# Row tiles leave PSUM by a copy and an adding DMA; the copies of y into PSUM go

## The chip, the cores and the metric

One core of a Trainium2 chip. The metric is the device time of one execution in microseconds (us). A core has five engines with a queue of their own: PE (matmul, with its weight loads listed as PEld), DVE (elementwise), ACT (copies and activations), POOL and SP, which mostly issue DMAs. PSUM holds the matmuls' sums in eight banks of 128 x 512 float32; SBUF holds everything else.

## The reference

A transformer layer over 256 positions of width 2048, float32, with two SwiGLU feed-forward halves around a mixer:

```python
def _swiglu(x, w_gate, w_up, w_down):
    return (jax.nn.silu(x @ w_gate) * (x @ w_up)) @ w_down
def _macaron_ffn(x, pre_g, w_gate, w_up, w_down, post_g):
    return x + 0.5 * _rms_norm(_swiglu(_rms_norm(x, pre_g), w_gate, w_up, w_down), post_g)
...
h = _macaron_ffn(h, ffn1...)       # D_MODEL 2048, D_FF 5632
h = _gated_mixers(h, ...)          # attention, Fourier mix, gates, output projection
h = _macaron_ffn(h, ffn2...)
```

The change lies in the two feed-forward halves alone.

## The kernel before

Every float32 product is made of three matmuls (`mm3`, lines 109 to 111): each operand is split into a high part (ACT, line 103, `whi`) and a low part (DVE, line 104, `wlo`). A split takes one piece of weights, 128 x 1024, which SP loads into one of five `raw` buffers (line 84).

A feed-forward half has its 5632 inner columns in 11 blocks of 512. The first two are done plainly. For each further block f, `ffn` feeds two things to a queue, `Line`:

- the **round**, the down-projection of an earlier block's h: y (256 x 2048) += h (256 x 512) @ w_down. It has four column blocks `cb` of 512 and, in each, two row tiles t = 0, 1 of 128 x 512, one PSUM bank each, two pieces of weights per column block. In class `Rows`, `seed(cb, t)` takes a bank and copies y into it (ACT, line 661, `pr<-y`), the matmuls add to it, and `out` copies it back to y (ACT, line 679, `y<-pr`). The seeds of a column block are issued at the first piece of the one before it.
- `swiglu`, gate and up of block f. Six of its eight pairs of weight rows use seven products in place of eight (`seven`); their weights are differences of loaded pieces (DVE, line 582, tile `t13`). Two pairs are plain. Sums in the banks p1, p5, p6, p7, g0, g1, u0, u1 (all eight banks, named `pc` in the trace) are put together at the end by the lists `sums` (with `copy` of p1 to x1 on ACT, line 591), `gates` and `ups` (DVE, lines 587 and 599; ACT, line 595), and leave the banks free for the next round.

`Line` keeps up to ten pieces ahead of PE (`RING` 6 and `RING_B8` 4; six in the last block): `feed` first pops the oldest entry (its matmuls, then its `then` list), then prepares the new one (load and split). An entry with `hold` lets the next feed's preparation wait for one step. DVE, ACT and PE run the loop in exactly the order in which it is written, so an ACT or DVE instruction that waits holds up all that stand behind it on its engine. PSUM has two pools: five banks `pmm` and three `ptr`. Work tiles (x1, x2, x3, x5) come from a pool of eight, `wk`.

At `cb == 3` of a round, the h of the block just finished is transposed on PE for the next round (`ahead`). There are ten such rounds in each half; the first has nothing to add to, the last is followed by `last_rows`, which does the eleventh block.

Of the kernel before, what the change touches and what calls it, by code (L numbers as in the profile page):

```python
# [10 lines left out]
F32 = mybir.dt.float32  # L11
# [3 lines left out]
AF = mybir.ActivationFunctionType  # L15
# [3 lines left out]
P = 128  # L19
D = 2048  # L20
# [37 lines left out]
def encoder_layer(  # L58
# [298 lines left out]
    def cbs(a, cb):  # L357
        return a[:, cb * NB:(cb + 1) * NB]
# [148 lines left out]
    def ring(src):  # L507

        n = src.shape[1]
        i = turn["n"] = (turn["n"] + 1) % (RING + RING_B8)  # L510
        if turn["more"] and i % 5 in (1, 3):
            both = big("w2", F32R, [P, 2, WP, NB])
            hi, lo = both[:, 0], both[:, 1]
        else:
            hi = wring.tile([P, WP, NB], F32R, tag="hi", name="whi")
            lo = wring.tile([P, WP, NB], F32R, tag="lo", name="wlo")
        split(hi[:, 0:n, :], lo[:, 0:n, :], src)
        return [(hi[:, i, :], lo[:, i, :]) for i in range(n)]

    def raw_piece(src, i):  # L520
        raw = wraw.tile([P, WP, NB], F32, tag="raw", name="raw")
        load(raw[:], src.rearrange("p (i k c) -> p i k c", k=WP, c=NB)[:, i])
        return raw
# [31 lines left out]
            while self.queue:  # L555
                self.next()

    def swiglu(line, forms, w, hs, seed):


        ps, begun, x = {}, set(), {}

        def mul(n, a, b, last=False):
            if n not in ps:
                ps[n] = ptr.tile([P, NB], F32, tag="tr", name="pc") if n in ("p5", "p7", "p1") else                     pmm.tile([P, NB], F32, tag="mm", name="pc")
            mm3(ps[n][:], *a, *b, n not in begun, last)
            begun.add(n)

        def raw(pair, i):
            return raw_piece(w[pair // 2], pair % 2 * 2 + i)  # L570

        def plain(pair, i, *then, hold=False):
            def use(b):
                for t in range(NT):
                    for j in range(2):
                        k = 2 * pair + j
                        mul("gu"[i] + str(t), forms.plain[k][t], b[j], k == KD - 1)

            line.feed(lambda: ring(raw(pair, i)[:]), use, *then, hold=hold)

        def minus(out, a, b):
            V.tensor_tensor(out=out, in0=a, in1=b, op=ALU.subtract)  # L582

        def add(out, a, b):
            if out not in x:
                x[out] = work(out)
            V.tensor_tensor(out=x[out][:], in0=ps[a][:], in1=x[b][:], op=ALU.add)  # L587

        def copy():
            x["x1"] = work("x1")  # L590
            A.activation(x["x1"][:], ps["p1"][:], AF.Copy)

        def silu(t):
            g = x["x" + "13"[t]]
            A.activation(g[:], g[:], AF.Silu)  # L595

        def times(t):
            g, up = x["x" + "13"[t]], x["x" + "25"[t]]
            V.tensor_tensor(out=up[:], in0=up[:], in1=g[:], op=ALU.mult)
            hs.append(up)  # L600

        def seven(pair, between=None, *then):
            a11, a12, na22, s1, s2, s3, s4 = forms.seven[pair]
# [12 lines left out]

            def second():
                b = ring(h["t"][:])
                minus(h["t"][:, 0, :], h["ra"][:, 1, :], h["rb"][:, 1, :])
                return b  # L620

            def two(n, a, m, b, last):
                def use(ws):
                    mul(n, a, ws[0], last)
                    mul(m, b, ws[1], last)
                return use

            line.feed(first, two("u0", s4, "g0", a12, False))
            line.feed(second, two("p5", s1, "p7", s3, end))
            if between:  # L630
                between()
            line.feed(lambda: ring(h["ra"][:]), two("p1", a11, "p6", s2, end), *then[0:4], hold=end)
            line.feed(lambda: ring(h["t"][:, 0:1, :]), lambda ws: mul("g1", na22, ws[0]), *then[4:], hold=end)

        sums = [copy, lambda: seed(0, ptr, "tr"), lambda: add("x2", "p6", "x1"), lambda: seed(1),
                lambda: add("x3", "p7", "x2"), lambda: add("x2", "p5", "x2"), lambda: add("x5", "p5", "x3")]
        gates = [lambda: add("x1", "g0", "x1"), lambda: add("x3", "g1", "x3"), lambda: silu(0), lambda: silu(1)]
        ups = [lambda: add("x2", "u0", "x2"), lambda: times(0), lambda: add("x5", "u1", "x5"), lambda: times(1)]
        for kg in range(KD // CK):
            a, b = 2 * kg, 2 * kg + 1  # L640
            if kg == KD // CK - 1:
                seven(a, None, *sums)
                plain(b, 0, *gates, hold=True)
                plain(b, 1, *ups)
            elif b in BY_SEVEN:
                seven(a)
                seven(b)
            else:
                seven(a, lambda: plain(b, 0))
                plain(b, 1)  # L650

    class Rows:


        def __init__(self, w, rb, y, first):
            self.w, self.rb, self.y, self.first, self.ps = w, rb, y, first, {}

        def seed(self, cb, t, pool=pmm, tag="mm"):
            self.ps[cb, t] = pool.tile([P, NB], F32, tag=tag, name="pr")
            if not self.first:  # L660
                A.activation(self.ps[cb, t][:], cbs(self.y[t], cb), AF.Copy)  # L661

        def feed(self, line, ch, ahead):

            def use(b, cb, i):
                if i == 0:
                    if cb in ahead:
                        ahead[cb]()
                    for t in range(NT if cb + 1 < D // NB else 0):
                        self.seed(cb + 1, t)  # L670
                for t in range(NT):
                    for j in range(WP):
                        k = i * WP + j
                        mm3(self.ps[cb, t][:], ch[0][:, k, t * P:(t + 1) * P], ch[1][:, k, t * P:(t + 1) * P], *b[j],
                            self.first and k == 0, k == CK - 1, not self.first)

            def out(cb):
                for t in range(NT):
                    A.activation(cbs(self.y[t], cb), self.ps[cb, t][:], AF.Copy)

            for cb in range(D // NB):
                for i in range(CK // WP):
                    line.feed(lambda i=i, cb=cb: ring(raw_piece(self.w[self.rb, cb], i)[:]),
                              lambda b, i=i, cb=cb: use(b, cb, i), *([lambda cb=cb: out(cb)] if i == CK // WP - 1 else []))

    def ffn(u, rs, wg, wu, wgu, wd, yname, tail, gate0, w_next=None, early=()):

# [29 lines left out]
        with tc.manual_schedule(engines={mybir.EngineType.DVE, mybir.EngineType.Activation, mybir.EngineType.PE}):  # L717
            for f in range(PLAIN, nblk + 1):
                if f == nblk:
                    norm, nxt = tail(y)  # L720

                def ahead(hs=hs, f=f):
                    chs.append(new_chunk("hT")) if f > PLAIN else None
                    turn_h(chs[-1], hs)

                before = {D // NB - 1: ahead}
                if f == PLAIN:
                    before[0] = lambda: forms.chunk(KD // CK - 1)
                if f == PLAIN:
                    rows = Rows(wd, 0, y, True)  # L730
                    for t in range(NT):
                        rows.seed(0, t)
                rows.feed(line, chs[-1] if f > PLAIN else chs[0], before)
                if f < nblk:
                    hs = []
                    rows = Rows(wd, f - 1, y, False)
                    turn["more"] = f < nblk - 1
                    swiglu(line, forms, wgu[f - PLAIN], hs, lambda t, *room, rows=rows: rows.seed(0, t, *room))
            line.end()
        return last_rows(chs[-1], wd, nblk - 1, y, norm, nxt, w_next), nxt  # L740

# [616 lines left out]
```

## Time and profile before

| | |
|---|---|
| median of 3 runs | 2140.59 us (2136.44 to 2143.92) |
| the profiled execution | 2148.34 us, its span 2146.6 us |
| mean granted PE clock | 0.971 |
| PE, DVE, ACT, POOL busy | 95%, 83%, 63%, 1% of the span |
| DMA | 417.46 MB, mean 194 GB/s |

A row of the trace names the line, the engine, the operation, and out<-in by tile names. `L661` is a line of this kernel. "Idle before" and the waits name the instruction that ended an engine's idle time. PEclk is the share of its full clock that PE was granted. Line numbers are those of the kernel before; in the changed one, the copies out are on lines 675 and 678, the adding DMA on 679, the last round's add on 681.

### The profile page before, as it was taken

What the parts mean: (1) busy time and instruction counts of PE and PEld (TensorE: products, weight loads), DVE (VectorE), ACT (ScalarE), POOL (GpSimd) and SP (SyncE); (2) the same over time, 40 slices, a digit from 0 to 9 for tenths busy, and PEclk for the clock granted to TensorE, in tenths of its full rate; (3) what the DMA queues carried; (4) which work ended last, traced back from release to release, by engine and by line L of the source; (5) the groups of instructions that cost most, each with busy time, mean ns of one, the idle gap of its engine ahead of it and who ended that gap; (6) DMA issues with size and microseconds to landing.
All of it is one profiled execution on the core that took longest, in us unless ns stands there. A gap on an engine that the chain in (4) does not pass through costs nothing.

```text
span 2146.6 us, 26154 instructions
## 1 busy us (share of the span) xinstructions
PE 2032.8 (95%) x9146; PEld 1669.9 (78%) x9146; DVE 1790.8 (83%) x2416; ACT 1360.3 (63%) x1940; POOL 28.6 (1%) x30
## 2 busy tenths in 40 slices
PE   9998889888989999999999999999899889988998
PEld 7877778777878778888888888888677777777876
DVE  6898898889888888876877895888888889888895
ACT  7666666666666766555666655655656665666666
POOL 0000000000000010100000000000000000000002
PEclk9999999999999999999999999999999999999999
DMA  8564565446547686864555557565554555455653
GB/s 315 188 195 156 176 214 180 149 163 216 179 148 258 228 264 215 243 213 143 185 192 183 185 181 272 194 206 168 191 184 159 174 189 186 159 179 189 234 191 134
DMA packets 118741, 417.46 MB, mean 194 GB/s; under 512 B 12969, under 2 KB 19121, under 8 KB 116433
## 3 DMA queue, kind: packets, MB, share of 16 engines
q1 hardware_dynamic: 114256, 411.66, 57.1%
q0 software_dynamic: 4352, 4.13, 1.3%
q8 instruction: 72, 1.18, 0.2%
q14 instruction: 61, 0.49, 0.1%
HBM read 409.44 MB, written 6.29 MB: 194 GB/s over the span
## 4 chain that ended last, share of the span: by engine, by line
PE 62%; DVE 25%; DMA 5%; ACT 4%; issue 3%; SPq 0%; DVEq 0%; ACTq 0%
PE pc L110 11%; PE pc L111 11%; PE pc L109 11%; DVE wlo L104 10%; PE pr L109 8%; PE pr L110 8%; PE pr L111 8%; DVE t L582 4%; DVE w L104 4%; DVE x L587 3%; DMA raw<-in_f_down 3%; ACT whi L103 2%; DVE raw L582 1%; PE pt L179 1%; ACT x L595 1%
## 5 line engine op out<-in xcount | busy, mean ns | idle before, releaser
L104 DVE TENSOR_TENSOR wlo<-raw,whi 128x1024 fp32r<-128x1024 f32 (+1 forms) x560 | 677.1, 1219 | 152.9 <-ACT whi L103 150.3
L103 ACT ACTIVATE whi<-raw 128x1024 fp32r<-128x1024 f32 (+1 forms) x560 | 585.3, 1055 | 298.6 <-PE pc L111 126.8
L109 PE MATMUL pc<-whi,uh 128*128 128x512 f32 x688 | 272.6, 396 | 0.8 <-ACT uh L764 0.8
L110 PE MATMUL pc<-wlo,uh 128*128 128x512 f32 x688 | 270.4, 393 | 0.8 <-DVE wlo L104 0.8
L111 PE MATMUL pc<-whi,ul 128*128 128x512 f32 x688 | 270.2, 393 | 0.0
L109 PE MATMUL pr<-whi,hTh 128*128 128x512 f32 x492 | 206.3, 419 | 63.7 <-ACT pr L661 63.5
L110 PE MATMUL pc<-wlo,fh 128*128 128x512 f32 x626 | 244.4, 390 | 1.2 <-DVE wlo L104 1.0
L109 PE MATMUL pc<-whi,fh 128*128 128x512 f32 x626 | 243.9, 390 | 0.7 <-DVE hTl L104 0.7
L111 PE MATMUL pc<-whi,fl 128*128 128x512 f32 x626 | 243.8, 389 | 0.0
L582 DVE TENSOR_TENSOR t<-raw 128x512 f32<-128x512 f32 x324 | 213.6, 686 | 3.8
L104 DVE TENSOR_TENSOR w<-raw,w 128x1024 fp32r<-128x1024 f32 x151 | 184.3, 1220 | 29.1 <-ACT w L103 28.5
L103 ACT ACTIVATE w<-raw 128x1024 fp32r<-128x1024 f32 x151 | 159.2, 1054 | 68.7 <-DMA raw<-in_f_down 21.9
L110 PE MATMUL pr<-wlo,hTh 128*128 128x512 f32 x492 | 201.4, 409 | 0.0
L111 PE MATMUL pr<-whi,hTl 128*128 128x512 f32 x492 | 200.9, 408 | 0.0
L103 ACT ACTIVATE whi<-t 128x1024 fp32r<-128x1024 f32 (+1 forms) x138 | 117.0, 848 | 99.2 <-DVE t L582 88.5
L109 PEld LDWEIGHTS pr<-whi,hTh 128*128 128x128 f32 x492 | 98.6, 200 | 92.9 <-ACT pr L661 71.1
L104 DVE TENSOR_TENSOR wlo<-t,whi 128x1024 fp32r<-128x1024 f32 (+1 forms) x138 | 132.0, 957 | 44.8 <-ACT whi L103 44.8
L109 PEld LDWEIGHTS pc<-whi,uh 128*128 128x128 f32 x688 | 130.1, 189 | 28.2 <-ACT uh L764 2.5
L110 PEld LDWEIGHTS pc<-wlo,uh 128*128 128x128 f32 x688 | 130.0, 189 | 28.0 <-DVE wlo L104 2.8
L111 PEld LDWEIGHTS pc<-whi,ul 128*128 128x128 f32 x688 | 129.9, 189 | 27.0
L110 PEld LDWEIGHTS pc<-wlo,fh 128*128 128x128 f32 x626 | 117.5, 188 | 27.9 <-DVE wlo L104 3.7
L109 PEld LDWEIGHTS pc<-whi,fh 128*128 128x128 f32 x626 | 117.5, 188 | 26.0 <-issue 0.8
(361 smaller groups left out, 3609.4 us busy)
## 6 DMA issues: line engine op xcount, KB each, us to landing
raw<-in_f_gu SPq DMA_DIRECT2D x288, 512.0 KB, 4.5
raw<-in_f_down SPq DMA_DIRECT2D x176, 512.0 KB, 5.3
raw<-in_w_in SPq DMA_DIRECT2D x112, 512.0 KB, 4.7
raw<-in_f_up SPq DMA_DIRECT2D x32, 512.0 KB, 4.7
raw<-in_w_ao SPq DMA_DIRECT2D x32, 512.0 KB, 4.0
raw<-in_w_out SPq DMA_DIRECT2D x32, 512.0 KB, 4.4
raw<-in_f_gate SPq DMA_DIRECT2D x31, 512.0 KB, 5.8
fraw<-in_w_f SPq DMA_DIRECT2D x16, 512.0 KB, 6.1
```

Of the source, the lines that this page charges most:

```text
L103: a = A.activation(hi, src, AF.Copy)
L104: v = V.tensor_tensor(out=lo, in0=src, in1=hi.bitcast(F32), op=ALU.subtract)
L109: T.matmul(ps, lh, rh, start=first, stop=False, skip_group_check=onto)
L110: T.matmul(ps, lh, rl, start=False, stop=False, skip_group_check=onto)
L111: return T.matmul(ps, ll, rh, start=False, stop=last, skip_group_check=onto)
L179: T.transpose(pt[:, j, :], src[:, j * P:(j + 1) * P], ident[:])
L582: V.tensor_tensor(out=out, in0=a, in1=b, op=ALU.subtract)
L587: V.tensor_tensor(out=x[out][:], in0=ps[a][:], in1=x[b][:], op=ALU.add)
L595: A.activation(g[:], g[:], AF.Silu)
```

## The change

The seeds go. The round's matmuls start a fresh sum in their bank. What leaves the bank goes to y in one of three ways: the first round copies it to y on ACT (as before); rounds two to nine copy it on ACT to a new tile `part` from the pool `wk`, and a DMA issued on POOL adds `part` to y in SBUF; the tenth adds it to y on DVE. Banks are now taken at a column block's own first piece, and by a table: tiles (0,0), (1,0) and (1,1) from `ptr`, where p1, p7 and p5 were, the others from `pmm`. The lists of the last `seven` are cut elsewhere: two entries of `sums` follow its third piece, which no longer holds, the rest follows the fourth.

```diff
-    def swiglu(line, forms, w, hs, seed):
+    def swiglu(line, forms, w, hs):
...
-            line.feed(lambda: ring(h["ra"][:]), two("p1", a11, "p6", s2, end), *then[0:4], hold=end)
-            line.feed(lambda: ring(h["t"][:, 0:1, :]), lambda ws: mul("g1", na22, ws[0]), *then[4:], hold=end)
-
-        sums = [copy, lambda: seed(0, ptr, "tr"), lambda: add("x2", "p6", "x1"), lambda: seed(1),
-                lambda: add("x3", "p7", "x2"), lambda: add("x2", "p5", "x2"), lambda: add("x5", "p5", "x3")]
+            line.feed(lambda: ring(h["ra"][:]), two("p1", a11, "p6", s2, end), *then[0:2])
+            line.feed(lambda: ring(h["t"][:, 0:1, :]), lambda ws: mul("g1", na22, ws[0]), *then[2:], hold=end)
+
+        sums = [copy, lambda: add("x2", "p6", "x1"), lambda: add("x3", "p7", "x2"), lambda: add("x2", "p5", "x2"),
+                lambda: add("x5", "p5", "x3")]
...
-        def seed(self, cb, t, pool=pmm, tag="mm"):
-            self.ps[cb, t] = pool.tile([P, NB], F32, tag=tag, name="pr")
-            if not self.first:
-                A.activation(self.ps[cb, t][:], cbs(self.y[t], cb), AF.Copy)
...
+    def row_line(line, ch, w, rb, y, way, ahead):
+        rooms = {(0, 0): (ptr, "tr"), (1, 0): (ptr, "tr"), (1, 1): (ptr, "tr")}
+        for cb in range(D // NB):
+            ps = []
+            def use(b, i, cb=cb, ps=ps):
+                if i == 0:
+                    if cb in ahead:
+                        ahead[cb]()
+                    for t in range(NT):
+                        pool, tag = rooms.get((cb, t), (pmm, "mm"))
+                        ps.append(pool.tile([P, NB], F32, tag=tag, name="pr"))
...
+            def out(t, cb=cb, ps=ps):
+                dst = cbs(y[t], cb)
+                if way == "set":
+                    A.activation(dst, ps[t][:], AF.Copy)
+                elif way == "dma":
+                    part = work("part")
+                    A.activation(part[:], ps[t][:], AF.Copy)
+                    nc.gpsimd.dma_start(dst, part[:], accum_op=ALU.add)
+                else:
+                    V.tensor_tensor(out=dst, in0=ps[t][:], in1=dst, op=ALU.add)
...
+                way = "set" if f == PLAIN else "dma" if f < nblk else "add"
+                row_line(line, chs[-1] if f > PLAIN else chs[0], wd, f - 2, y, way, before)
```

ACT at the border between a block and its round, in the middle of the first half, before: the copy of p1, the two seeds of column block 0, two silus, four splits (`whi`, `w2` are split weights, `t13` the differences), the seeds of column block 1, and the first copies out.

```order
L591 ACTIVATE x1_3659<-pc_3396 128x512
L661 ACTIVATE pr_3661<-y0_941 128x512
L661 ACTIVATE pr_3665<-y1_942 128x512
L595 ACTIVATE x1_3659<-x1_3659 128x512
L595 ACTIVATE x3_3670<-x3_3670 128x512
L103 ACTIVATE whi_3709<-raw_3707 128x1024
L103 ACTIVATE w2_3715<-raw_3713 128x1024
L103 ACTIVATE whi_3725<-raw_3720 128x1024
L103 ACTIVATE whi_3730<-t13_3722 128x1024
L661 ACTIVATE pr_3735<-y0_941 128x512
L661 ACTIVATE pr_3737<-y1_942 128x512
L103 ACTIVATE w2_3751<-raw_3718 128x1024
```

The same place on ACT now:

```order
L591 ACTIVATE x1_3691<-pc_3428 128x512
L103 ACTIVATE whi_3697<-raw_3695 128x1024
L595 ACTIVATE x1_3691<-x1_3691 128x512
L595 ACTIVATE x3_3704<-x3_3704 128x512
L103 ACTIVATE w2_3743<-raw_3741 128x1024
L103 ACTIVATE whi_3753<-raw_3748 128x1024
L103 ACTIVATE whi_3758<-t13_3750 128x1024
L103 ACTIVATE w2_3777<-raw_3746 128x1024
L678 ACTIVATE part_3792<-pr_3763 128x512
L678 ACTIVATE part_3795<-pr_3764 128x512
L103 ACTIVATE whi_3798<-t13_3750 128x512
```

No copy from y is left, one split stands between the copy of p1 and the silus, and the copies out write `part`.

DVE at the same border, before: the last split ahead of the sums, the first five sums.

```order
L104 TENSOR_TENSOR w2_3650<-raw_3648,w2_3650 128x1024
L587 TENSOR_TENSOR x2_3663<-pc_3400,x1_3659 128x512
L587 TENSOR_TENSOR x3_3670<-pc_3388,x2_3663 128x512
L587 TENSOR_TENSOR x2_3663<-pc_3384,x2_3663 128x512
L587 TENSOR_TENSOR x5_3673<-pc_3384,x3_3670 128x512
L587 TENSOR_TENSOR x1_3659<-pc_3375,x1_3659 128x512
```

And now:

```order
L104 TENSOR_TENSOR w2_3682<-raw_3680,w2_3682 128x1024
L587 TENSOR_TENSOR x2_3693<-pc_3432,x1_3691 128x512
L104 TENSOR_TENSOR wlo_3698<-raw_3695,whi_3697 128x1024
L587 TENSOR_TENSOR x3_3704<-pc_3420,x2_3693 128x512
L587 TENSOR_TENSOR x2_3693<-pc_3416,x2_3693 128x512
L587 TENSOR_TENSOR x5_3707<-pc_3416,x3_3704 128x512
```

One split has moved from behind the sums to behind the first of them; the rest of DVE's order in the block is the same. PE's order doesn't change. POOL, which issued nothing in the feed-forward halves, now issues eight of these per round (the first two of a round are shown):

```order
L679 DMA y0_941<-part_3792 128x512
L679 DMA y1_942<-part_3795 128x512
```

They stand in the order of the copies on ACT, whose tiles they read.

More of the change, by code (lines that the diff above doesn't have):

```diff
@@ L650, in swiglu @@
                 plain(b, 1)
-    class Rows:
-        def __init__(self, w, rb, y, first):
-            self.w, self.rb, self.y, self.first, self.ps = w, rb, y, first, {}
-        def seed(self, cb, t, pool=pmm, tag="mm"):
-            self.ps[cb, t] = pool.tile([P, NB], F32, tag=tag, name="pr")
-            if not self.first:
-                A.activation(self.ps[cb, t][:], cbs(self.y[t], cb), AF.Copy)
-        def feed(self, line, ch, ahead):
-            def use(b, cb, i):
+    def row_line(line, ch, w, rb, y, way, ahead):
[3 more added lines that the diff above has]
+            def use(b, i, cb=cb, ps=ps):
                 if i == 0:
@@ L668, in use @@
                         ahead[cb]()
-                    for t in range(NT if cb + 1 < D // NB else 0):
-                        self.seed(cb + 1, t)
+                    for t in range(NT):
+                        pool, tag = rooms.get((cb, t), (pmm, "mm"))
+                        ps.append(pool.tile([P, NB], F32, tag=tag, name="pr"))
                 for t in range(NT):
@@ L673, in use @@
                         k = i * WP + j
[L674 to L684, printed above, removed]
+                        mm3(ps[t][:], ch[0][:, k, t * P:(t + 1) * P], ch[1][:, k, t * P:(t + 1) * P], *b[j],
+                            k == 0, k == CK - 1)
+            def out(t, cb=cb, ps=ps):
[8 more added lines that the diff above has]
+                    V.tensor_tensor(out=dst, in0=ps[t][:], in1=dst, op=ALU.add)
+            for i in range(CK // WP):
+                line.feed(lambda i=i, cb=cb: ring(raw_piece(w[rb, cb], i)[:]), lambda b, i=i, use=use: use(b, i),
+                          *([lambda t=t, out=out: out(t) for t in range(NT)] if i == CK // WP - 1 else []))
     def ffn(u, rs, wg, wu, wgu, wd, yname, tail, gate0, w_next=None, early=()):
@@ L728, in ffn @@
                     before[0] = lambda: forms.chunk(KD // CK - 1)
[L729 to L733, printed above, removed]
+                way = "set" if f == PLAIN else "dma" if f < nblk else "add"
+                row_line(line, chs[-1] if f > PLAIN else chs[0], wd, f - 2, y, way, before)
                 if f < nblk:
                     hs = []
-                    rows = Rows(wd, f - 1, y, False)
                     turn["more"] = f < nblk - 1
-                    swiglu(line, forms, wgu[f - PLAIN], hs, lambda t, *room, rows=rows: rows.seed(0, t, *room))
+                    swiglu(line, forms, wgu[f - PLAIN], hs)
             line.end()
```

## The prediction

> **What bounds the kernel now.** I read the page first, then the waits, then a table of stretches, then the timeline of one block border.
>
> ```profile
> PE 2032.8 (95%) x9146; PEld 1669.9 (78%) x9146; DVE 1790.8 (83%) x2416; ACT 1360.3 (63%) x1940; POOL 28.6 (1%) x30
> ```
>
> PE looks nearly full, so only its waits, its clock, or its amount of work can give time. In the list of waits (us in total, times, longest), all large waits of PE have one name:
>
> ```profile
> PEld pr L109 <- ACT pr L661: 103.5, 31, 6.6
> PE pr L109 <- ACT pr L661: 91.9, 19, 6.1
> ```
>
> L661 is the seed, the copy of y into a PSUM bank; PEld's wait is mostly the same time again. So PE stands 91.9 us before row tiles. The table of stretches (bounds in us, length; then busy time of PE, PEld, DVE, ACT, POOL with instruction counts; clock, DMA share, GB/s) shows where:
>
> ```profile
> core 0: us, PE busy (x) PEld busy (x) DVE busy (x) ACT busy (x) POOL busy (x), PEclk, DMA share, GB/s
> 162.83:660.81 497.98, 456.62 (x1947) 373.21 (x1947) 428.61 (x506) 319.07 (x399) 0.00 (x0) 0.94 0.53 178
> 1528.46:2027.06 498.60, 457.22 (x1947) 373.01 (x1947) 429.48 (x507) 318.47 (x400) 0.00 (x0) 0.95 0.54 178
> 446.47:471.96 25.49, 19.38 (x72) 15.33 (x73) 21.41 (x28) 16.09 (x23) 0.00 (x0) 0.87 0.40 131
> 660.81:677.19 16.38, 16.38 (x74) 13.46 (x73) 14.17 (x19) 12.46 (x19) 0.00 (x0) 1.00 0.96 347
> 386.88:408.57 21.69, 21.68 (x89) 17.77 (x90) 14.72 (x19) 15.16 (x24) 0.00 (x0) 0.88 0.34 106
> 408.57:434.15 25.58, 25.58 (x114) 21.20 (x113) 25.44 (x31) 15.91 (x18) 0.00 (x0) 1.00 0.51 170
> 434.15:446.47 12.32, 12.19 (x55) 9.77 (x53) 9.44 (x9) 8.26 (x9) 0.00 (x0) 1.00 0.92 326
> 386.88:458.36 71.48, 65.23 (x278) 53.09 (x279) 61.21 (x74) 45.60 (x58) 0.00 (x0) 0.95 0.53 178
> ```
>
> Rows 1 and 2 are seven rounds each of the two FFNs: 996.58/14 = 71.18 us per block. Row 3 is three column blocks of one round, row 4 the same work in the round that has no such wait: 25.49 against 16.38. The 9.11 us between them are 6.11 us idle and 3.00 us in which the same matmuls ran at half clock (PE busy 19.38 against 16.38, clock 0.87 against 1.00). Without both, a block is 71.18 - 9.11 = 62.1 us of PE.
>
> Why PE waits is in the timeline of the border at 446 us (start, duration). PE:
>
> ```profile
> 451.86 0.39 PE L111 MATMUL pr<-whi,hTl 128*128 128x512 f32 x1
> 458.36 0.79 PE L109 MATMUL pr<-w,hTh 128*128 128x512 f32 x1 [6.11 <-ACT pr L661]
> ```
>
> ACT and DVE in that time:
>
> ```profile
> 445.21 0.58 ACT L591 ACTIVATE x<-pc 128x512 f32<-128x512 f32 x1
> ...
> 450.98 1.05 ACT L103 ACTIVATE whi<-raw 128x1024 fp32r<-128x1024 f32 x1
> 451.93 1.04 ACT L103 ACTIVATE w<-raw 128x1024 fp32r<-128x1024 f32 x1
> 452.87 1.04 ACT L103 ACTIVATE whi<-raw 128x1024 fp32r<-128x1024 f32 x1
> 456.76 1.06 ACT L103 ACTIVATE whi<-t 128x1024 fp32r<-128x1024 f32 x1 [2.85 <-DVE t L582]
> 457.72 1.10 ACT L661 ACTIVATE pr<-y 128x512 f32<-128x512 f32 x2
> ```
>
> ```profile
> 446.48 4.53 DVE L587 TENSOR_TENSOR x<-pc,x 128x512 f32<-128x512 f32 x7
> ...
> 453.11 1.22 DVE L104 TENSOR_TENSOR wlo<-raw,whi 128x1024 fp32r<-128x1024 f32 x1
> ...
> 455.38 1.28 DVE L582 TENSOR_TENSOR t<-raw 128x512 f32<-128x512 f32 x2
> ```
>
> The two seeds of column block 1 stand on ACT behind four splits; the fourth waits for DVE's t, and DVE is busy with the block's ten sums and two splits first. Banks and split weights for column block 1 are there; only the seed is late.
>
> **What is late next: DVE.** A block's 61.21 us of DVE (last row above) are almost PE's 62.1, so its idle 10.27 us decide. Their causes, from the waits of the stretch 386.88:408.57:
>
> ```profile
> DVE wlo L104 <- ACT whi L103: 3.5, 3, 1.7
> ACT y L679 <- PE pr L111: 3.3, 6, 0.8
> ACT whi L103 <- PE pr L111: 1.6, 1, 1.6
> ```
>
> and of 434.15:446.47:
>
> ```profile
> ACT whi L103 <- DMA raw<-in_f_down: 2.6, 3, 2.0
> DVE wlo L104 <- ACT whi L103: 1.9, 1, 1.9
> DVE w L104 <- ACT w L103: 0.9, 1, 0.9
> ```
>
> In the first stretch DVE idles 21.69 - 14.72 = 6.97 us because ACT waits for a PE that comes late: this goes when PE comes early. In the second it idles 2.88 us because ten whole pieces are split in a row and their loads (DMA share 0.92, 326 GB/s) don't keep up: this stays. Between them (408.57:434.15) DVE is busy 25.44 of 25.58 us. So DVE's own pace is 71.48 - 6.97 = 64.5 us per block, slower than PE's 62.1.
>
> **The change part by part.**
>
> Seeds: 144 go, and with them PE's wait and half clock; ACT is relieved, but it wasn't the bound. The copy out stays, now into a part tile instead of y. Durations from the groups of instructions (the number behind the bar is busy us, then mean ns):
>
> ```profile
> L661 ACT ACTIVATE pr<-y 128x512 f32<-128x512 f32 x72 | 40.8, 593 | 7.4 <-DVE x L587 7.1
> L679 ACT ACTIVATE y<-pr 128x512 f32<-128x512 f32 x80 | 46.1, 592 | 26.7 <-PE pr L111 26.6
> L587 DVE TENSOR_TENSOR x<-pc,x 128x512 f32<-128x512 f32 x144 | 92.5, 684 | 1.2
> ```
>
> ACT per block: 8 x 0.59 = 4.7 us less, worth nothing by itself.
>
> Banks: tile (0,0) now needs ACT's copy x1 (at 445.21 here, ready before PE's row start at 446.47), (0,1) DVE's first sum, (1,0) the second, (1,1) the fourth, then g0, g1, u0, u1. DVE's seven sums end at 451.0 while PE's first column block ends at 452.3, so PE finds each free if DVE is as early as here. One split moves between the first sum and the rest: the rest come 1.2 us later, the total is the same. SP's loads keep their order; the load of that split is wanted one step earlier, still in the burst that loads can't follow, but DVE has a sum to do meanwhile.
>
> Sum for the 14 rounds: PE could do 62.1, DVE 64.5, and the ring of ten pieces can lend PE only the few us that copy x1 is early (446.47 - 445.79 = 0.7 us), so the slower one sets the pace: 14 x (71.18 - 64.5) = 93.5 us.
>
> Other seed waits: 91.9 - 14 x 6.1 = 6.5 us at the first and last rounds. Those at the first stand behind the same copy x1, so I take 3 of 6.5.
>
> The last round's 16 adds on DVE: 16 x 0.684 = 10.9 us, at best beside PE (0), at worst all on the path. Each add waits for PE to finish its tile, and DVE's next splits are queued behind it; but DVE leads PE there, and seeds leave ACT, so I take 2.
>
> The accumulating DMAs: 128, eight per block, 256 KB each, issued by POOL. Nearest rows, the 16 accumulating loads of the mixer (252 KB), the queues, and a stretch with four of them:
>
> ```profile
> L897 POOL DMA_DIRECT2D fraw<-in_w_f x16: 1078/1092/1230, 770.6 to 920.9; - x16
> DMA to landing us min/median/max: 4.1/6.7/10.9
> q1 hardware_dynamic: 114256, 411.66, 57.1%
> q0 software_dynamic: 4352, 4.13, 1.3%
> 897.00:921.00 24.00, 24.00 (x125) 20.35 (x124) 19.30 (x23) 13.08 (x15) 3.38 (x4) 1.00 0.91 269
> ```
>
> POOL: 8 x 1.1 = 9 us per block on an engine with nothing else to do in the FFNs; each issue waits for its copy on ACT, and only the next issue is queued behind it: hidden. DMA engines: 1.3% of 2146.6 us over 4.13 MB is 6.8 us per MB, against 3.0 for loads; 2.1 MB per block cost 14.2 us of all 16 engines. With today's 0.53 x 71.2 = 37.7 that is 52 of 64.5 us: room over the block. Locally, beside the parts' landing, loads ask 0.51 x 25.6 = 13 us, together 27 in 25.6. Bounds: nothing (in the last row PE stays 24.00 of 24.00 busy at share 0.91), or DVE's wait for loads doubles, 14 x 2.8 = 39 us. I take nothing, by that row, which is the same kind of DMA. A gain is excluded, since no transfer goes.
>
> Landing: part tiles share eight buffers with x1 to x5; a round's last two parts reuse those of its first two, three column blocks (16.4 us) later. At most 10.9 us of landing hides there.
>
> Here a rule speaks against the change: the Trainium skill, "SBUF — State Buffer", section "Who interferes with whom", says that descriptors of a DMA issued on POOL can starve while DVE holds a port that the two share, but counts tensor_tensor out of that. The rows agree with the exception: 1.08 to 1.23 us per issue, though DVE was busy 19.30 of 24.00 us. By the rows the sum stays as below; by the rule without its exception the slower rival would come true.
>
> Total: 93.5 + 3 - 2 = 94.5; 2148.34 (profiled execution) - 94.5 = 2053.8. That execution is 7.75 us above the median of the runs, 2140.59, so on the median's scale 2046.
>
> **Rivals.**
> - *PE sets the pace.* DVE's load wait shrinks or the ring lends more: 14 x 9.11 + 6.5 = 134 us, 2007. For it: the round without a wait ran at PE's full speed. Against: DVE at 25.44 of 25.58.
> - *DMA contention.* The added traffic makes the splits' loads late, twice the 2.8 us: 2046 + 39 = 2085. For it: share 0.92 in the burst already. Against: parts land earlier in the block.
> - *Slower: parts land too late.* If POOL's issues starve, a round's last copies on ACT wait for the first parts' landing, and all splits stand behind them. It begins at 16.4 us and eats the gain of 6.7 us per round at 23 us; at 25 us the time is 2140.6 + 14 x 2 = 2169. Against: twice the longest landing seen.
> - *The wait only changes its name.* PE then waits at the row's start for copy x1 or the sums, as long as for the seed: no change. Against: the seven sums that free the banks end at 451.0, today's seeds start at 457.7.
>
> **How the numbers follow.** DVE's pace 0.58 (2025 to 2065), PE's pace 0.17, contention 0.17 (2065 to 2095), same 0.03, slower 0.05. Time 2046; the range takes in both rivals' prices: 2007 to 2085. The three runs of before lie within 0.35%, so 0.3% (6 us) is about what can be told from no change: faster 0.92, same 0.03, slower 0.05.
>
> **What would show it.** No L661; no 6 us wait of PE in rounds; clock near 1.00 there; DVE over 90% busy per block, and a block of 64 to 65 us; short waits of PE (2.4 us per block) for L591's x1, sums or splits; DMA share near 0.8; parts landing under 12 us. Wrong if blocks are near 62 (DVE had more room), or over 67 with splits waiting for loads, or if ACT waits for y's DMAs.

## The result and the profile after

The changed kernel takes 2073.36 us, median of 4 runs (2068.56 to 2076.93), beside 2141.94 us for the kernel before (median of 4): the ratio is 0.9682, 95% interval 0.9655 to 0.971, or 68.6 us less. The profiled execution of it took 2068.56 us, its span is 2066.6 us. The page of the profile, its first part and its queues:

```profile
PE 2005.2 (97%) x9146; PEld 1652.5 (80%) x9146; DVE 1792.5 (87%) x2432; ACT 1265.4 (61%) x1780; POOL 140.4 (7%) x158
...
q1 hardware_dynamic: 114256, 411.66, 58.1%
q0 software_dynamic: 22784, 37.69, 10.3%
...
raw<-in_f_gu SPq DMA_DIRECT2D x288, 512.0 KB, 5.1
...
y<-part POOLq DMA_DIRECT2D x64, 256.0 KB, 8.2
...
yf<-part POOLq DMA_DIRECT2D x64, 256.0 KB, 7.8
```

The stretches that answer to those of before (two times seven rounds, then one block alone; columns as in the prediction's table):

```profile
163.27:626.30 463.03, 443.60 (x1946) 364.25 (x1946) 425.48 (x505) 284.04 (x344) 48.93 (x56) 0.99 0.73 223
1487.65:1948.45 460.80, 445.23 (x1946) 365.21 (x1946) 425.30 (x505) 283.45 (x344) 48.80 (x56) 0.98 0.73 224
295.96:362.42 66.46, 62.41 (x278) 51.38 (x279) 60.85 (x73) 40.58 (x50) 7.00 (x8) 1.00 0.72 221
```

923.83/14 = 65.99 us per block, where it was 71.18. These 14 blocks give 14 x 5.19 = 72.7 us of the 79.8 us between the two profiled executions (2148.34 and 2068.56); the other 7.1 us lie in the first and last rounds and around them. DVE is busy 92% of the stretch (425.48 of 463.03) and idle 37.55/7 = 5.4 us per block, before 9.9 (497.98 - 428.61, over 7).

The waits (us in total, times, longest), with those for the loads of the gate/up weights:

```profile
PEld pr L109 <- ACT x L591: 44.9, 16, 4.5
ACT whi L103 <- DMA raw<-in_f_gu: 44.6, 12, 6.0
...
PE pr L109 <- ACT x L591: 38.0, 16, 4.0
...
DVE t L582 <- DMA raw<-in_f_gu: 26.0, 14, 3.0
...
ACT w L103 <- DMA raw<-in_f_gu: 20.7, 5, 5.2
```

L661 is gone. PE now waits for copy x1 (L591) at the row start, 38.0 us in all against 91.9 for the seeds. And a wait is new: DVE's t (the differences that the seven products need) waits for a load, 26.0 us in 14 waits, one in each of the 14 blocks, each about 35 us after the block's row start; ACT's two waits for the same loads were 18.4 and 9.2 us before. DVE and then ACT in the timeline of the block that starts at 295.96:

```profile
328.63 0.69 DVE L582 TENSOR_TENSOR t<-raw 128x512 f32<-128x512 f32 x1
331.26 0.69 DVE L582 TENSOR_TENSOR t<-raw 128x512 f32<-128x512 f32 x1 [1.94 <-DMA raw<-in_f_gu]
```

```profile
331.34 1.06 ACT L103 ACTIVATE w<-raw 128x1024 fp32r<-128x1024 f32 x1 [4.95 <-DMA raw<-in_f_gu]
```

What the DMA engines did in the 19 us up to there, 311 to 330, in 40 slices (busy tenths, then GB/s), with the queues' shares of that stretch:

```profile
DMA  2976999999999999999999999999999999999999
GB/s 26 138 207 198 328 289 224 220 285 388 358 276 207 203 211 203 198 207 207 272 358 379 254 241 289 306 310 341 246 224 203 216 198 203 207 242 367 401 397 431
...
q0 software_dynamic: 1143, 2.08, 60.9%
q1 hardware_dynamic: 776, 2.86, 43.2%
```

From the fifth slice on the engines are never free, and yet move only about 200 GB/s for long stretches and close to 400 in others. The eight adding DMAs of the block (2.08 MB on q0) take 60.9% of 19 us, 11.6 us of all engines; the loads get 2.86 MB through.

### The profile page after: what moved, and what is told of

Its sections match the earlier page's. It is cut to its first block, busy times and chain, and to the rows that moved or that the text cites. A ratio compares the mean times of both kernels' runs of the same rounds, so it can differ in the third digit from the quotient of the medians.

```text
span 2066.6 us, 26436 instructions
## 1 busy us (share of the span) xinstructions
PE 2005.2 (97%) x9146; PEld 1652.5 (80%) x9146; DVE 1792.5 (87%) x2432; ACT 1265.4 (61%) x1780; POOL 140.4 (7%) x158
## 4 chain that ended last, share of the span: by engine, by line
PE 54%; DVE 28%; DMA 10%; issue 4%; ACT 4%; SPq 0%; ACTq 0%; DVEq 0%
DVE wlo L104 11%; PE pc L110 9%; PE pc L111 8%; PE pc L109 8%; PE pr L109 8%; PE pr L110 7%; PE pr L111 7%; DVE t L582 6%; DVE w L104 5%; DMA raw<-in_f_down 5%; DMA raw<-in_f_gu 3%; DVE raw L582 2%; ACT whi L103 2%; PE pt L179 1%; DVE x L587 1%
## 5 line engine op out<-in xcount | busy, mean ns | idle before, releaser
L109 PE MATMUL pr<-whi,hTh 128*128 128x512 f32 x492 | 197.0, 400 | 21.8 <-ACT x L591 21.8
L104 DVE TENSOR_TENSOR w<-raw,w 128x1024 fp32r<-128x1024 f32 x151 | 184.2, 1220 | 18.4 <-ACT w L103 17.9
L110 PE MATMUL pr<-wlo,hTh 128*128 128x512 f32 x492 | 194.1, 395 | 0.0
L111 PE MATMUL pr<-whi,hTl 128*128 128x512 f32 x492 | 194.1, 395 | 0.0
L111 PEld LDWEIGHTS pc<-whi,fl 128*128 128x128 f32 x626 | 117.5, 188 | 24.2
```

What stands on the lines that cost most here:

```text
L104: v = V.tensor_tensor(out=lo, in0=src, in1=hi.bitcast(F32), op=ALU.subtract)
L109: T.matmul(ps, lh, rh, start=first, stop=False, skip_group_check=onto)
L110: T.matmul(ps, lh, rl, start=False, stop=False, skip_group_check=onto)
L111: return T.matmul(ps, ll, rh, start=False, stop=last, skip_group_check=onto)
```

## The experiments

The theory: DVE sets the pace once the seeds are gone, and part of the gain is lost because the adding DMAs delay the loads of gate/up. The first rival: the loss is the moved split and bank order, seen in PE's wait for copy x1. Medians of the kernel before in these comparisons were 2142.56 to 2144.49 us. e1, e3, e8 and e9 leave out part of the sum over the rounds, so they show a price and don't replace the kernel.

**e1, no adding DMA.**

```
                     A.activation(part[:], ps[t][:], AF.Copy)
-                    nc.gpsimd.dma_start(dst, part[:], accum_op=ALU.add)
```

> The changed kernel, with the copy into a part tile but without the DMA that adds it to y: the sum over the rounds' blocks is left out (y keeps round f=2's tiles and the last round's), 128 DMAs of 256 KB are gone. Theory (DVE sets the pace; the eight adding DMAs of a round make the loads of the next gate/up weights late, about 2.4 us of DVE per block): DVE's wait for the loads of gate/up at +33 us into a block goes, blocks fall from 66.0 to about 64 us, the whole from 2073 to 2035 to 2050. Rival A (the missing part is the bank order: PE stands 1.2 to 4.0 us at each row start for copy x1 and then runs at half clock): no change, 2068 to 2078, and the wait of DVE stays. Rival B (PE sets the pace, 62.1 us): 14 x 4 = 55 us less, about 2018.

Measured: 2035.99 us, ratio 0.9501 (0.9484 to 0.9518). Its first seven rounds, and its waits:

```profile
163.12:608.40 445.28, 438.20 (x1946) 360.75 (x1946) 424.06 (x505) 283.87 (x344) 0.00 (x0) 1.00 0.59 199
```

```profile
ACT whi L103 <- DMA raw<-in_f_gu: 19.6, 9, 2.4
...
PE pr L109 <- ACT x L591: 16.1, 15, 2.3
...
DVE t L582 <- DMA raw<-in_f_gu: 0.6, 1, 0.6
```

445.28/7 = 63.61 us per block, 2.4 less than with the adding DMAs, and 2073.36 - 2035.99 = 37.4 us in all. DVE's wait falls from 26.0 to 0.6 us, ACT's first from 44.6 to 19.6, and PE's wait for copy x1 from 38.0 to 16.1 although the bank order and the moved split are still there: more than half of that wait (21.9 of 38.0 us) was a consequence of late loads. Rival A fell as the cause of the loss; 16.1 us of its wait remain. In this kernel PE is busy 62.6 of 63.6 us and DVE 60.6, so the two stand close together.

**e2, DVE adds.**

```
-                way = "set" if f == PLAIN else "dma" if f < nblk else "add"
+                way = "set" if f == PLAIN else "add"
```

> The changed kernel with each row tile added to y by DVE in every round (as the last round does it) instead of copy and DMA: 8 x 0.684 = 5.5 us more of DVE per block, 4.7 us less of ACT, no adding DMA. Theory (DVE sets the pace): about 60.9 + 5.5 + 2.9 = 69.3 us per block against 66.0, so 14 x 3.3 = 46 us longer and some more in the other rounds, 2115 to 2130. Rival A (DVE's idle 5 us per block would take the adds): within 8 us of 2073. Rival B (adds that wait for PE hold back the splits queued behind them): over 72 us per block, slower than the kernel before, 2150 or more.

Measured: 2103.66 us, ratio 0.982 (0.9803 to 0.9838), faster than expected, but far from rival A.

```profile
161.72:640.07 478.35, 451.43 (x1947) 370.65 (x1947) 457.46 (x561) 260.83 (x288) 0.00 (x0) 0.96 0.55 185
```

```profile
PEld pt L179 <- DVE yf L681: 28.1, 8, 4.3
PEld pt L179 <- DVE y L681: 26.6, 7, 4.0
```

A block is 478.35/7 = 68.34 us, 4.7 more than e1; DVE's busy time grew by (457.46 - 424.06)/7 = 4.8. So DVE's added work lies on the path almost whole: DVE's idle time, 3.0 us per block in e1, is still 3.0 here. PE shows it as a wait of its transposes (L179) behind the adds. The expectation came out too high by 1.0 us per block. It took 5.5 us for eight adds, where busy time grew by 4.8 (one add lasts 0.68 us as expected, but overlaps its neighbours in time, as is shown below), and it started from the DVE busy time of the changed kernel, 60.9 us, where e1 has 60.6.

**e3, the same DMAs without adding.**

```
-                    nc.gpsimd.dma_start(dst, part[:], accum_op=ALU.add)
+                    nc.gpsimd.dma_start(dst, part[:])
```

> The changed kernel with the same 128 DMAs as plain copies of the part tile onto y, without adding: the sum over the blocks is left out, the transfers have the same source, destination and size. If what delays the loads is that adding packets are slow on the DMA engines (178 ns for 2 KB, against 159 ns for a load's 4 KB), the packets fall to about half and the time comes to between 2045 and 2065; if the traffic or the queue itself delays them, it stays at 2068 to 2078; by rival A (copy x1 at the row start) it stays there too.

Measured: 2037.94 us, ratio 0.9509 (0.9493 to 0.9526): the interval overlaps e1's, so the same bytes as a plain copy cost nothing that can be told from no DMA at all. From its page:

```profile
q0 software_dynamic: 14592, 37.69, 5.5%
...
raw<-in_f_gu SPq DMA_DIRECT2D x288, 512.0 KB, 4.5
...
y<-part POOLq DMA_DIRECT2D x64, 256.0 KB, 5.7
```

The queue held 4352 packets and 1.3% before the change. The 128 copies add 10240 packets and 4.2% of 2038.2 us, 86 us of all engines; the 128 adding DMAs add 18432 packets and 9.0% of 2066.6 us, 186 us, for the same 33.56 MB. They land after 8 us instead of 5.7. The stretch of e3 that answers to 311 to 330 of the changed kernel (15 to 34 us after the start of the round in its block):

```profile
DMA  8796899999999695879999999996115689997998
...
q1 hardware_dynamic: 914, 3.36, 60.1%
q0 software_dynamic: 640, 2.10, 27.8%
```

The copies carry the same 2.1 MB in less than half the engines' time, the loads get 3.36 MB through in place of 2.86, and DVE's wait for them is not in e3's list. It is the adding, not the traffic or POOL's queue, that is paid.

An adding DMA's packets are also smaller. In the trace they carry 2 KB and take 178 ns (median), those of the plain copy 4 KB and 159 ns. Size alone hardly explains it: in the kernel before, packets of plain loads of 2 KB take 84 ns and of 1024 bytes 46 ns, packets of the mixer's adding loads of 1008 bytes 102 ns. So at about the same size an adding packet takes about twice the time of a plain one; the plain ones come from HBM, and no run copied SBUF to SBUF in packets of 2 KB.

One page bears on this: the Trainium skill, "Collectives: The Full Stack", section "Stop ④ — SDMA + CCE: where bytes move and the add happens", tells of a small ALU in the path of the DMA engines and of a reduction that comes as "read-read-write with the add free in between". Free there is the add, not the second read, which a plain copy doesn't have. By e3 and the changed kernel an adding DMA takes 2.2 times the engines' time of a plain one; whether the read or the add is paid, no run here tells.

**e4, the kernel before with two seeds moved.** In the kernel before, column block 1's seeds go among the sums, into p7's and p5's banks, and no longer stand at the first piece of column block 0 (the main part of the edit is shown):

```
-        sums = [copy, lambda: seed(0, ptr, "tr"), lambda: add("x2", "p6", "x1"), lambda: seed(1),
-                lambda: add("x3", "p7", "x2"), lambda: add("x2", "p5", "x2"), lambda: add("x5", "p5", "x3")]
+        sums = [copy, lambda: seed(0, 0, ptr, "tr"), lambda: add("x2", "p6", "x1"), lambda: seed(0, 1),
+                lambda: add("x3", "p7", "x2"), lambda: seed(1, 0, ptr, "tr"), lambda: add("x2", "p5", "x2"), lambda: add("x5", "p5", "x3"), lambda: seed(1, 1, ptr, "tr")]
```

> The kernel before, with its seeds, but the two seeds of column block 1 are issued among the block's seven sums, into the banks of p7 and p5, instead of behind four splits. No DMA that adds, no other edit. Theory (the gain of the change was to free PE's row start of the late seed; the adding DMAs are a cost): the 6 us wait goes, blocks come to 64 to 65 us without the load wait in the middle, 2040 to 2060, faster than the changed kernel. Rival A (ACT's 4.7 us of seeds per block are on the path, or the seed wait only moves to the seeds of the next column block): blocks of 68 us or more, 2100 or more. Rival C (loads are late there in any kernel whose blocks are shorter, with or without adding DMAs): about 66 us per block, 2070 to 2080.

Measured: 2103.7 us, ratio 0.9819 (0.9803 to 0.9834). The theory's number missed, rival A's second half came true: the wait moved from column block 1 to column block 2, where the next seeds still stand behind splits.

```profile
243.31 0.50 PE L109 MATMUL pr<-whi,hTh 128*128 128x512 f32 x1 [3.88 <-ACT pr L661]
```

The round started at 228.25; a column block takes 5.4 us of PE, so 243.31, after the wait, is the first matmul of column block 2. Seven blocks take 475.02 us, 67.9 each.

**e5, all seeds early.** As e4, with column block 2's seeds after the silu and column block 3's after the last products:

```
-        gates = [..., lambda: silu(0), lambda: silu(1)]
-        ups = [..., lambda: add("x5", "u1", "x5"), lambda: times(1)]
+        gates = [..., lambda: silu(0), lambda: silu(1), lambda: seed(2, 0), lambda: seed(2, 1)]
+        ups = [..., lambda: add("x5", "u1", "x5"), lambda: times(1), lambda: seed(3, 0), lambda: seed(3, 1)]
...
-                    for t in range(NT if cb + 1 < D // NB else 0):
+                    for t in range(NT if cb + 1 < D // NB and self.first else 0):
```

> The kernel before, with all eight seeds of a round issued at the block's end, each as soon as a bank's sum has left it (column block 1 in p7 and p5, column block 2 in g0 and g1 behind the silu, column block 3 in u0 and u1), so that none stands behind a split. In the run before (e4, column block 1 alone) the wait had moved to the seeds of column block 2, 3.7 to 3.9 us and a half clock after it. Theory: the seeds as such cost nothing, only their place did; without adding DMAs the blocks come to where they are without them (63.6 us in e1), with up to 1 us more for 4.7 us of ACT before its splits: 2036 to 2056, faster than the changed kernel. Rival A (ACT's seeds ahead of the splits make the first splits late, and DVE waits): 2070 to 2090. Rival D (the wait moves on again, to column block 3 or the next row start, at 3 us and more per round): 2095 or more.

Measured: 2054.38 us, ratio 0.9594 (0.9579 to 0.961), inside the theory's range, 19 us faster than the changed kernel.

```profile
162.26:614.26 452.00, 441.31 (x1947) 361.87 (x1947) 425.27 (x505) 315.30 (x399) 0.00 (x0) 0.99 0.57 195
```

```profile
PE pr L109 <- ACT pr L661: 27.4, 15, 3.4
```

64.57 us per block with all 144 seeds of the kernel before: of 7.6 us between the kernel before and e1, their place cost 6.6. The other 1 us per block is what they still cost ahead of the splits. Part of it is a wait of PE that remains: at the row start the first seed stands directly behind copy x1, and PE waits for it 27.4 us in all, where it waits 16.1 for the copy in e1.

**e6 and e7, the rest of the change.** In the changed kernel, e6 puts the third piece's hold back, e7 takes the two tiles of column block 1 from other banks:

```
-            line.feed(lambda: ring(h["ra"][:]), two("p1", a11, "p6", s2, end), *then[0:2])
+            line.feed(lambda: ring(h["ra"][:]), two("p1", a11, "p6", s2, end), *then[0:2], hold=end)
```

```
-        rooms = {(0, 0): (ptr, "tr"), (1, 0): (ptr, "tr"), (1, 1): (ptr, "tr")}
+        rooms = {(0, 0): (ptr, "tr")}
```

> The changed kernel with the third piece's hold put back, so that the one split per block that had moved between DVE's first two sums stands behind all ten again; bank order and adding DMAs stay. Theory (DVE and PE run close together, adding DMAs are the lost part): DVE's sums end 1.2 us earlier, its split 9 us later, hidden by the ring: 2068 to 2085. Rival A (the moved split makes PE's row start late): the wait for copy x1 does not hang on it, but the banks do; if it was this, 14 x 1.2 = 17 us faster, 2056. Rival E (the early split is half of the gain, as it lets PE pass the third piece): 2100 or more.

> The changed kernel with column block 1's two row tiles taken from the banks of g0 and g1 instead of p7 and p5 (only tile (0,0) still takes p1's); DVE's and ACT's order stay the same. Theory (DVE's sums free every bank before PE's column block 1 starts 6 us into the round): no change, 2068 to 2079; PE shows no wait at column block 1. Rival (g0's and g1's sums come 5th and 6th, after the moved split, and make PE wait at column block 1): 1 to 3 us per round, with half clock 2 to 6: 2100 or more.

Measured: 2074.36 us (ratio 0.969, 0.9673 to 0.9706) and 2076.54 us (0.9697, 0.9683 to 0.9712). Neither differs from the changed kernel (0.9655 to 0.971). The moved split and the choice of these two banks neither gained nor lost, and e7's list has no wait of PE for a late sum.

**e8 and e9, which adding DMAs cost.** The adding DMA for column blocks 0 and 1 alone, and for 2 and 3 alone:

```
-                    nc.gpsimd.dma_start(dst, part[:], accum_op=ALU.add)
+                    if cb < 2:
+                        nc.gpsimd.dma_start(dst, part[:], accum_op=ALU.add)
```

(e9: `cb > 1`.)

> The changed kernel with the adding DMA for column blocks 0 and 1 alone; the tiles of column blocks 2 and 3 are copied to a part and not added (their sum over the rounds is left out). Half of the 128 adding DMAs remain. Theory F (each adding DMA costs the same, by the share of the DMA engines it takes): half of 2073 - 2036 = 37 us, 2050 to 2058. Theory G (it is a collision: those of column blocks 2 and 3 land where the gate/up loads for +33 us are under way, those of 0 and 1 land in time): 2034 to 2045, and no wait of DVE for gate/up loads. Theory H (those of 0 and 1 collide with the burst of whole pieces): 2065 or more.

> The counterpart of e8: the adding DMA for column blocks 2 and 3 alone, 64 of 128; the sum over the rounds of column blocks 0 and 1 is left out. Theory G (the collision is that of column blocks 2 and 3 with the gate/up loads): all of the cost is back, 2066 to 2078, with DVE's waits for gate/up loads. Theory F' (each of the last four is costly only because four others of its kind are still in the queue ahead of it): 2040 to 2055.

Measured: 2037.96 us (ratio 0.9515, 0.9501 to 0.9529) and 2050.85 us (0.9562, 0.9548 to 0.9576). So column blocks 0 and 1 alone cost 2 us above e1, which can't be told from nothing; 2 and 3 alone cost 15; all eight cost 37. Theory G holds for e8 but not whole for e9: its range was missed, and F' hit. The parts are not additive. That the second four meet the first four when there are all eight is read from the slices. The same 19 us of a block (15 to 34 us after the row start), first e8, then e9:

```profile
DMA  0199398999999999999999999611000398899999
...
q1 hardware_dynamic: 913, 3.35, 52.5%
q0 software_dynamic: 576, 1.05, 30.4%
```

```profile
DMA  8869798620000098479999999999999999999999
...
q1 hardware_dynamic: 914, 3.36, 51.9%
q0 software_dynamic: 576, 1.05, 30.7%
```

Both still have idle slices, and the loads move 3.35 MB; in the changed kernel there are none, and they move 2.86. DVE's wait for them, in e9 (e8's list has no such wait):

```profile
DVE t L582 <- DMA raw<-in_f_gu: 5.2, 7, 1.7
```

**e10, e11 and e12, a mixture.** Column blocks 0 and 1 by adding DMA, 2 and 3 seeded early:

```
-        gates = [..., lambda: silu(0), lambda: silu(1)]
+        gates = [..., lambda: silu(0), lambda: silu(1), lambda: [room(2, t, True) for t in range(NT)]]
...
+        def room(cb, t, seed=False, more=True):
+            if more or not seed:
+                ready[cb, t] = pmm.tile([P, NB], F32, tag="mm", name="pr")
+                if seed:
+                    A.activation(ready[cb, t][:], cbs(y[t], cb), AF.Copy)
...
-                        mm3(..., k == 0, k == CK - 1)
+                        mm3(..., k == 0 and not seeded[cb], k == CK - 1, seeded[cb])
...
-                if way == "set":
+                if way == "set" or seeded[cb]:
```

e10 seeds column block 3 behind `times(1)`; e11 and e12 at the start of column block 2:

```
+                    if cb == 2 and way == "dma":
+                        room(3, 0, True), room(3, 1, True)
```

> The changed kernel with column blocks 0 and 1 copied and added by DMA, and column blocks 2 and 3 seeded from y (start from y's value in PSUM, copied back to y by ACT), their four seeds behind the block's silu and last products, ahead of the splits; tile (0,1)'s bank taken when p6's sum has left it. Four adding DMAs per round, four seeds. Theory G with e5's reading (adding DMAs of column blocks 0 and 1 are free, a seed ahead of the splits costs 1 us per 8): between e8's 2038 and e5's 2054, 2040 to 2050. Rival (seeds of u0's and u1's banks come late in the block, and the splits behind them hold DVE as in e5): as e5, 2054 or more.

> As e10, but column block 3's two seeds issued where the kernel before has them, at the start of column block 2. Theory: they stand behind splits there, but PE needs them only 5.4 us later (no wait of PE for column block 3 in e4), and two seeds less stand ahead of the first splits: 2036 to 2046, 1 to 8 us below e10. Rival (in the shorter block the splits ahead of them are late, and PE waits at column block 3): 2060 or more.

Measured: 2141.57 us (ratio 0.9987, 0.9978 to 0.9997) and 2101.84 us (0.9803, 0.9783 to 0.9822). The theory's numbers failed in both, and the wait is not the one that either rival named. PE of e10, and what DVE did then:

```profile
162.92 0.50 PE L109 MATMUL pr<-whi,hTh 128*128 128x512 f32 x1 [2.56 <-ACT x L591]
...
164.18 0.39 PE L111 MATMUL pr<-whi,hTl 128*128 128x512 f32 x1
170.54 0.79 PE L109 MATMUL pr<-whi,hTh 128*128 128x512 f32 x1 [5.97 <-DVE x L587]
```

```profile
165.29 3.80 DVE L587 TENSOR_TENSOR x<-pc,x 128x512 f32<-128x512 f32 x6
169.19 0.69 DVE L599 TENSOR_TENSOR x<-x,x 128x512 f32<-128x512 f32 x1
169.80 0.68 DVE L587 TENSOR_TENSOR x<-pc,x 128x512 f32<-128x512 f32 x1
```

After six matmuls, where tile (0,1) begins, PE waits for a sum that ends at 170.48: the last of the eight that read a bank, u1's. So, by this wait, (0,1) stood in u1's bank; in e11, with two seeds fewer ahead of it, it waited for an earlier sum, 3 to 4 us. The seeds write their tiles before PE writes (0,1), and it seems that they took p6's bank and those after it. e12 tests that:

```
-        rooms = {(0, 0): (ptr, "tr"), (1, 0): (ptr, "tr"), (1, 1): (ptr, "tr")}
+        rooms = {(0, 0): (ptr, "tr"), (0, 1): (ptr, "tr"), (1, 0): (ptr, "tr")}
...
-            line.feed(lambda: ring(h["ra"][:]), two("p1", a11, "p6", s2, end), *then[0:2])
+            line.feed(lambda: ring(h["ra"][:]), two("p1", a11, "p6", s2, end), *then[0:2], hold=end)
```

> As e11 (column blocks 0 and 1 added by DMA, 2 and 3 seeded, column block 3's seeds at the start of column block 2), with other banks: tiles (0,0), (0,1) and (1,0) take those of p1, p7 and p5, the rest those of p6, g0, g1, u0, u1, and the third piece's hold is put back, so that p7's sum comes 0.7 us after p6's. In e10 and e11 PE stood 3 to 6 us inside column block 0, where its second tile begins, until a late sum of DVE. Theory I (there the second tile had been given a bank whose sum is late, since the seeds, written first, took the early ones): that wait shrinks to under 1 us, blocks 63.7 to 64.5 us, 2036 to 2050. Rival J (it is the seeds: they hold ACT, hence the splits, hence DVE's sums): the wait stays at 3 us or more, 2090 or more.

Measured: 2037.75 us (2035.28 to 2038.06), ratio 0.9504 (0.9487 to 0.952), 35.6 us faster than the changed kernel and as fast as e1, which has no adding DMA at all.

```profile
160.96:605.80 444.84, 439.25 (x1947) 361.45 (x1948) 426.15 (x506) 299.13 (x371) 24.55 (x28) 1.00 0.68 216
```

```profile
PE pr L109 <- ACT pr L724: 9.6, 12, 0.9
...
PE pr L109 <- ACT x L591: 5.1, 3, 2.4
...
DVE t L582 <- DMA raw<-in_f_gu: 0.2, 1, 0.2
```

63.55 us per block; PE is busy 98.7% of it, and what it still waits for after the first of these rounds is mostly column block 3's seeds (L724), 0.9 us at most. e12 keeps the whole sum. It changed banks and hold together, but the hold by itself moved nothing in e6, so the banks are what e10 and e11 lacked. Which bank each tile has is worked out from the waits; no view shows it.

## Why the prediction was right, and which terms were mis-sized

The direction was right, and so was the main mechanism, the late seeds. The term for the adding DMAs was not: 2046 was forecast and 2073.36 came, inside the range, but where the contention rival stood (2065 to 2095, chance 0.17) and not the likeliest case (2025 to 2065). A block of 66 us lies between the 64 to 65 that were to show the forecast and the 67 that were to refute it. Two smaller terms, DVE's pace and the first and last rounds, erred the other way and covered about half of the miss (12.6 and 6 of 37 us), which is luck.

- *Seeds removed: PE's wait and half clock go.* Right, and shown from both sides: 63.61 us per block without seeds and without adding DMAs (e1), 64.57 with all seeds in an earlier place (e5).
- *DVE's pace of 64.5 us per block.* Too slow by 0.9: e1 ran at 63.61, e12 at 63.55. Two pieces: in e1 DVE was busy 60.6 us, not 61.2, and idle 3.0, not 3.3. Over 14 blocks that is 12.6 us that the sum left out. The 0.6 us are mostly overlap: an instruction of DVE that needn't wait begins before the one ahead of it has ended, by some 0.08 us (in the changed kernel, 310.35 + 1.22 = 311.57, and the next begins at 311.48):

```profile
310.35 1.22 DVE L104 TENSOR_TENSOR wlo<-raw,whi 128x1024 fp32r<-128x1024 f32 x1
311.48 0.68 DVE L104 TENSOR_TENSOR wlo<-t,whi 128x512 fp32r<-128x512 f32 x1
```

  Busy time counts the overlap once. In seven rounds of before 364 of 505 instructions overlap the one ahead so, in e1's 410 of 504, since DVE waits less often; one alone lasts the same within 4 ns. That makes 3.5 of the 4.6 us in seven rounds. So a wait cost DVE its idle time and about 0.08 us more, which the sum didn't have. That DVE's work lies on the path was right (e2: 4.7 of 4.8 us), but PE, busy 62.6 us, is only 1 us behind.
- *Adding DMAs: "I take nothing, by that row".* This step failed: they cost 37.4 us, almost the upper bound of 39. The mechanism of that bound, loads late and DVE's wait for loads near twice, is what the trace shows, only that the late loads are those of gate/up 33 us into the block and not the burst at its end. The row that was chosen has four adding loads in 24 us, which carry 0.77 MB and take 21.3% of the engines there, and e8, with the four of column blocks 0 and 1, also cost nothing. Eight that are issued within 12 us (310.64 to 322.38 in the block shown) and take 60.9% of 19 us are another case. The prediction's own local sum, 27 us of DMA work in a stretch of 25.6, had said that the room was gone.
- *Its price per MB* was somewhat high: 6.8 us of all engines, measured 186/33.56 = 5.5.
- *First and last rounds: 3 gained, 2 lost.* Measured 7.1 gained. No run took the last round's adds by themselves, so how these 6 us divide is open.
- *Bank order and moved split: nothing.* Right (e6, e7).
- *POOL's issues: hidden.* Right: 48.93 us for 56 issues, 0.87 us each, while DVE was busy 92% of the stretch. With the tensor_tensor instructions that DVE runs there, the starving of descriptors that the prediction weighed is not seen; landing took 8.1 us in the median and 13.2 at most, over the 12 that were named as a sign and under the 16.4 at which the slower rival begins.
- *The wait only changes its name.* In part: PE waits for copy x1, 38.0 us in all. Short waits of this kind were among the prediction's signs, 2.4 us per block, and 38.0 in 16 waits is 2.4 each. With the same banks and without late loads the wait is 16.1 (e1), 21.4 (e3) and 17.8 us (e8), so about half of it was the echo of late loads.

The sum with the measured terms, between the profiled executions, on which it was made: 94.5 + 12.6 + 6 = 113 us without the adding DMAs, where e1's execution (2034.3) lies 114.0 below 2148.34. The DMAs take 34.3 of that back (2068.56 - 2034.3; by the medians 37.4), which leaves the 79.8 us between the two executions. By the medians it is 68.6 us, as the profiled execution of before lies 6.4 us above its median and that of the changed kernel 4.8 below.

## What to carry to other kernels

A late operation that stalls an engine can often be cured by its place alone: e5 got 88 of the 107 us that e1 shows by issuing the same copies earlier, with no other engine or queue. Before work is moved onto the DMA engines, sum what they are asked for in the stretch where it lands, not over the block, and keep adding transfers sparse: here the four of column blocks 0 and 1 were free, the four of 2 and 3 cost 15 us, and all eight 37. When instructions are moved ahead of others, look at which banks they take from those that are needed first.

## What the runs showed of the hardware that was not expected

- An adding DMA of 256 KB, SBUF to SBUF, makes 144 packets, the plain one 80 (18432 and 10240 over 128), and takes 2.2 times the engines' time: 5.5 against 2.6 us of all 16 engines per MB.
- POOL needs 0.87 us to issue the adding DMA, and 0.54 us for the plain one (30.07 us for 56 in e3):

```profile
162.07:607.03 444.96, 436.92 (x1947) 359.61 (x1947) 423.98 (x505) 283.88 (x344) 30.07 (x56) 1.00 0.68 232
```

- The plain copies share the engines with the loads at 232 GB/s in these rounds, and the block stays at 63.57 us; with adding ones it is 65.99 at 223 GB/s. The mean share, 0.68 against 0.73, hardly tells the two apart; the local stretch does: q0 takes 27.8% of it for 2.10 MB, against 60.9% for 2.08.
